# A second out_proj cut in two, with the queries and scores of the gathered block between its halves

## Chip, cores and metric

The kernel runs on one core of one Trainium2 chip. The metric is the device time of one execution in microseconds (us); the lower the better. Three timed runs of the kernel before gave 2075.72, 2077.70 and 2087.32 us, so the median is 2077.7 us. TE below stands for TensorE, the other engines are called as in the profile: PE (TensorE matmul), PEld (its weight loads), DVE (VectorE), ACT (ScalarE), POOL (GpSimd), SP (SyncE, which here only issues DMAs; SPq, ACTq are the queues of those engines).

## What is computed

One layer of a diffusion backbone over 512 latent tokens (four blocks of 128, numbered l = 0 to 3) with a prefix of 256 context tokens. Only its second half matters here. The output of the two token mixers goes through one output projection, then through a layer in which every token fetches 8 x 16 single-neuron experts out of 16384 (PEER):

```python
x = x + gt1 * merge_branches(...)          # the last step in it: y @ w_out, w_out is 1024 x 1024
h2 = rmsnorm(x, norm_ffn) * (1 + sc2) + sh2
# per block of 128 tokens:
q = (hb @ w_q).reshape(128, 8, 2, 64)                       # queries, 8 heads
s = einsum('thpd,hpkd->thpk', q, keys)                      # scores, 2 x 128 keys a head
half_s, half_i = top_k(s, 16)                               # selection, first stage
best_s, best_c = top_k(all 16 x 16 sums, 16)                # selection, second stage
experts = i1 * 128 + i2;  gate = softmax(best_s)
act = gelu(einsum('td,thkd->thk', hb, u_table[experts]))
out = einsum('thk,thkd->td', gate * act, v_table[experts])
```

The result is added to x and normalised. All matmuls of 1024 inputs are done in three products, hi*hi + hi*lo + lo*hi, of a rounded value and its remainder.

## The kernel before, in words

The kernel is written with a tile framework whose scheduler decides the order of the instructions on every engine: it takes what is ready by its own model of time, by priority, else in the order of the program. Each engine then works through its own list strictly in that order. What matters lies between the mixers and the loop over the experts:

- **Order of the program** (before): `out_proj(PAIRS[0])` for blocks 3 and 2, `out_proj(PAIRS[1])` for blocks 0 and 1, `transpose_h2` of the first pair, `queries(PAIRS[0])`, `scores(3)`, `transpose_h2` of the second pair, `run_topk(TK0)`, `queries(PAIRS[1])`, `run_topk(TK1)`, then `scores` of blocks 2, 0 and 1, and after that the loop.
- **out_proj** (L1274): eight steps k of 128 input channels. Each loads 512 KB of w_out into a `w_raw` tile (four buffers), `split` (L164 to L171) rounds it on ACT (L169, `w_hi`) and takes the remainder on POOL (L170, `w_lo`; three buffers each), and PE does 12 matmuls of 512 columns (L174 to L176) into four accumulators `pt`. After the eighth step a chain per block makes h2 of it: DVE L1295 (two products out of PSUM), L1296 (sum with `xr`), ACT L1299 (squares) and L1301 (root), DVE L1300, L1302, L1303 (`junk`) and L1304 (`h2t`).
- **transpose_h2** (L1309): PE L1315 transposes h2t, ACT L1318 rounds the result (`h2T_hi`), DVE L1319 takes the remainder (`h2T_lo`). The matmuls of `queries` read both.
- **queries** (L1322): per head a load of 512 KB of peer_wq in four DMAs, the same split, 24 matmuls of 256 columns, one copy on ACT (L1333).
- **scores** (L1335): per two heads one PSUM tile of scores (L1339), copied by ACT to `sce` (L1341) and stored to `scd` in DRAM (L1342).
- **The selection** `topk` (L1091) reads a block's scores back from `scd` (L1094) into `sc` and works on DVE alone: L1101 to L1105 (first stage), L1108 to L1118 (sums), L1126 to L1130 (second stage), then for each head three instructions of 800 elements (L1137, L1139, L1140) that look up the expert's number. Block LG = 3 is the one whose experts are gathered row by row with indirect DMAs (L1439, L1450); the other three are computed densely. `run_topk(us)` emits as much of the selection as a budget of `us` covers, with high priority: 10 (TK0) and 30 (TK1) before the loop, the rest piece by piece in the loop. These budgets count, they look at no clock: they cover all of block 3's selection but the last seven of its eight look-ups.
- **The loop** over 128 groups of experts begins with L1393 to L1397 (constants into PSUM and a tile), `transpose_u` (L1465 DVE, L1466 ACT, L1470 POOL) and `first_product` (PE, tile `pa`). From L1393 on the order of DVE and POOL is written by hand (`manual_schedule`). L1396 writes into memory that the `sce` tiles held, so it waits until their stores to DRAM have landed.

## Time and profile before

| | us |
|---|---|
| three timed runs | 2075.72, 2077.70, 2087.32 (median 2077.7) |
| the profiled execution, its own time | 2080.87 |
| its span from first to last instruction | 2079.1 |
| PE, DVE, ACT, POOL busy | 1928.9, 1643.1, 951.1, 976.9 |
| mean granted clock of TensorE | 0.969 |
| end of the first half of the second out_proj on PE | 710.1 |
| queries of blocks 3 and 2 on PE | 726.1 to 752 |
| queries of blocks 0 and 1 on PE | 758.4 to 784 |
| selection of block 3 before the loop, on DVE | 766.8 to 797.5 |
| first matmul of the loop | 802.3 |

The busy times are sums over the whole span; the change touches some 110 us of it, from 700 to 802. A row of a timeline reads: start, duration, engine, line, operation, tiles out<-in, shape, count, and in brackets how long the engine had been idle and what ended that wait. The durations of DVE and ACT rows include some 0.06 to 0.1 us in which the next instruction has already begun.

### The profile page before, as it was taken

The numbers are of one execution on the slowest core, as the hardware profiler recorded it, in microseconds if no ns is written. First come the engines' busy times: TensorE is split into PE (matmuls) and PEld (weight loads), VectorE is DVE, ScalarE is ACT, GpSimd is POOL, SyncE is SP. The second block draws the span as 40 slices with busy tenths as digits, with TensorE's granted clock in tenths as the row PEclk, the third lists the DMA queues.
The fourth block names the chain that finished last, engine by engine and source line by source line (L and its number), as shares of the span: only waits on it lengthen the run. The fifth ranks groups of instructions, "written<-read, shape, count | busy, mean of one in ns | idle before, by whom it ended". The sixth has DMA issues, their size and how long they took to land.

```text
span 2079.1 us, 29606 instructions
## 1 busy us (share of the span) xinstructions
PE 1928.9 (93%) x10018; PEld 1627.8 (78%) x10018; DVE 1643.1 (79%) x3304; ACT 951.1 (46%) x1769; POOL 976.9 (47%) x695
## 2 busy tenths in 40 slices
PE   6999999999897897999999999899889999999998
PEld 2766666788786696989999999888778777777786
DVE  4599885378776768799998999666879898989855
ACT  5545544333333443333766666895323333333333
POOL 2655534311212872677565666443445555555200
PEclk9999999999998998999999999999999999999999
DMA  9333322422515685889889878789999999999963
GB/s 308 92 112 116 107 82 81 127 84 63 138 51 182 201 195 158 234 234 252 242 255 266 246 236 256 242 259 309 300 315 376 386 386 393 389 391 397 352 233 107
DMA packets 283477, 475.87 MB, mean 229 GB/s; under 512 B 35224, under 2 KB 197293, under 8 KB 282813
## 3 DMA queue, kind: packets, MB, share of 16 engines
q1 hardware_dynamic: 214251, 277.82, 43.9%
q0 software_dynamic: 36864, 134.23, 18.9%
q10 hardware_dynamic: 32210, 61.93, 8.4%
q8 instruction: 79, 1.29, 0.3%
q14 instruction: 73, 0.60, 0.1%
HBM read 409.71 MB, written 64.18 MB: 228 GB/s over the span
## 4 chain that ended last, share of the span: by engine, by line
PE 36%; DMA 17%; DVE 14%; issue 14%; POOL 12%; ACT 5%; ACTq 1%; SPq 1%; DVEq 0%; POOLq 0%
DMA grow<-in_peer_v_dram,exi 7%; POOL w_lo L1470 7%; POOL grow L1439 3%; PE pg L176 3%; PE pg L175 3%; PE pg L174 3%; PE pacc L175 3%; PE pacc L176 2%; PE pacc L174 2%; PE pa L176 2%; PE pa L174 2%; PE pa L175 2%; DMA rep<-ad 2%; DVE accg L1454 2%; PE pm L1422 2%
## 5 line engine op out<-in xcount | busy, mean ns | idle before, releaser
L1470 POOL TENSOR_TENSOR w_lo<-ut,w_hi 128x512 fp32r<-128x512 f32 x224 | 293.9, 1335 | 231.4 <-ACT w_hi L1466 225.3
L174 PE MATMUL pa<-h2T_hi,w_hi 128*128 128x384 f32 x1024 | 354.6, 346 | 35.2 <-ACT w_hi L1466 32.4
L176 PE MATMUL pa<-h2T_hi,w_lo 128*128 128x384 f32 x1024 | 361.2, 354 | 9.3 <-POOL w_lo L1470 8.4
L175 PE MATMUL pa<-h2T_lo,w_hi 128*128 128x384 f32 x1024 | 349.9, 342 | 0.0
L170 POOL TENSOR_TENSOR w_lo<-w_raw,w_hi 128x1024 fp32r<-128x1024 f32 x78 | 200.1, 2576 | 305.1 <-ACT w_hi L169 229.3
L1450 POOL DMA_INDIRECT grow<-in_peer_v_dram,exi x128 | 200.0, 1563 | 168.0 <-DVE accg L1454 143.4
L1552 ACT CAST w_hi<-w_raw 128x1024 fp32r<-128x1024 f32 x124 | 130.3, 1051 | 226.3 <-DMA w_raw<-in_peer_v_dram 110.8
L175 PE MATMUL pacc<-w_lo,wh 128*128 128x512 f32 x744 | 214.0, 403 | 20.1 <-DVE w_lo L1556 19.5
L174 PEld LDWEIGHTS pa<-h2T_hi,w_hi 128*128 128x128 f32 x1024 | 198.3, 194 | 43.3 <-ACT w_hi L1466 42.8
L176 PEld LDWEIGHTS pa<-h2T_hi,w_lo 128*128 128x128 f32 x1024 | 197.8, 193 | 16.0 <-POOL w_lo L1470 13.1
L176 PE MATMUL pacc<-w_hi,wl 128*128 128x512 f32 x744 | 208.8, 396 | 0.0
L174 PE MATMUL pacc<-w_hi,wh 128*128 128x512 f32 x744 | 208.3, 395 | 0.0
L175 PEld LDWEIGHTS pa<-h2T_lo,w_hi 128*128 128x128 f32 x1024 | 197.5, 193 | 0.3
L1439 POOL DMA_INDIRECT grow<-in_peer_u_dram,exi x128 | 148.3, 1159 | 100.4 <-DVE act L1432 80.4
L175 PEld LDWEIGHTS pacc<-w_lo,wh 128*128 128x128 f32 x744 | 138.6, 190 | 63.0 <-DVE w_lo L1556 31.7
L1466 ACT CAST w_hi<-ut 128x1024 fp32r<-128x1024 f32 x126 | 132.6, 1053 | 114.6 <-DVE ut L1465 80.4
L1454 DVE SCALAR_TENSOR_TENSOR accg<-grow,act,accg 128x1024 f32<-128x1024 f32 x127 | 162.8, 1282 | 25.1 <-DMA grow<-in_peer_v_dram,exi 24.1
L1556 DVE TENSOR_TENSOR w_lo<-w_raw,w_hi 128x1024 fp32r<-128x1024 f32 x124 | 151.3, 1220 | 33.7 <-ACT w_hi L1552 33.7
L176 PEld LDWEIGHTS pacc<-w_hi,wl 128*128 128x128 f32 x744 | 140.6, 189 | 34.3
L174 PEld LDWEIGHTS pacc<-w_hi,wh 128*128 128x128 f32 x744 | 139.4, 188 | 34.7 <-ACT wh L1543 0.5
L1465 DVE STREAM_TRANSPOSE ut<-w_raw 128x1024 f32<-128x1024 f32 x126 | 155.8, 1238 | 10.7 <-DMA w_raw<-in_peer_u_dram 7.9
L174 PE MATMUL pg<-hL_hi,w_hi 128*128 128x512 f32 (+1 forms) x336 | 139.6, 416 | 0.0
(447 smaller groups left out, 4115.9 us busy)
## 6 DMA issues: line engine op xcount, KB each, us to landing
w_raw<-in_peer_u_dram SPq DMA_DIRECT2D x512, 128.0 KB
w_raw<-in_peer_v_dram SPq DMA_DIRECT2D x128, 512.0 KB
Gd<-stg ACTq DMA_DIRECT2D x48, 512.0 KB
gg<-Gd SPq DMA_DIRECT2D x16, 1536.0 KB
Ad<-ga ACTq DMA_DIRECT2D x112, 192.0 KB
aa<-Ad SPq DMA_DIRECT2D x28, 768.0 KB
w_raw<-in_w_ada_dram SPq DMA_DIRECT2D x40, 512.0 KB
w_raw<-in_w_in_dram SPq DMA_DIRECT2D x34, 512.0 KB
```

Of the source, the lines that this page charges most:

```text
L170: (lo_eng or G).tensor_tensor(lo, raw, hi.bitcast(F32), op=ALU.subtract)
L174: PE.matmul(o, lh, rh, start=start, stop=False)
L175: PE.matmul(o, lh, rl, start=False, stop=False)
L176: PE.matmul(o, ll, rh, start=False, stop=stop)
L1439: G.indirect_dma_start(out=u, out_offset=None, in_=UT_, in_offset=bass.IndirectOffsetOnAxis(ap=exi[:, j:j + 1], axis=0))
L1450: G.indirect_dma_start(out=v, out_offset=None, in_=VT_, in_offset=bass.IndirectOffsetOnAxis(ap=exi[:, j:j + 1], axis=0))
L1454: V.scalar_tensor_tensor(accg, v, act[:, j:j + 1], accg, op0=ALU.mult, op1=ALU.add)
L1465: V.transpose(lf.rearrange("p (c f q) -> p c f q", f=4, q=32), u.rearrange("p f (c x) -> p c f x", x=32))
L1466: S.copy(hi, lf)
L1470: eng.tensor_tensor(lo[:, cs], lf[:, cs], hi[:, cs].bitcast(F32), op=ALU.subtract)
L1552: S.copy(vh, v)
L1556: V.tensor_tensor(vl, v, vh.bitcast(F32), op=ALU.subtract)
```

## The change

- `out_proj` takes a range of steps. The second one, for blocks 0 and 1, is done in two calls: steps 0 to 3 before, steps 4 to 7 after `queries(PAIRS[0])` and `scores(3)`. Its four accumulators stay open between the halves; its chain for h2 follows the second half.
- `scores(LG)`: the copies of block 3's scores go from PSUM straight to the tile `sc` of the selection, and the four stores to `scd` and the load from it are gone. The scores of the other blocks still go through `scd`.
- The order of the program becomes: out_proj of 3 and 2, first half of 0 and 1, transposes of 3 and 2, queries of 3 and 2, scores of 3, second half of 0 and 1, transposes of 0 and 1, `run_topk(TK0)`, and on as before.

```diff
--- before.py
+++ after.py
@@ -1064,6 +1064,7 @@
     psa = psa_cm.__enter__()
     psm = [None, None]
     io = [iota]
+    kept = {}
     ready, now, spent, stage = {}, [0], [0.0, 0.0], [0]
     LG = NLB - 1
 
@@ -1090,8 +1091,9 @@
 
     def topk(l):
 
-        sc = tkt([P, HEADS, 2 * KEYS], "sc")
-        SP.dma_start(sc, scd[l])
+        sc = kept[l] if l in kept else tkt([P, HEADS, 2 * KEYS], "sc")
+        if l not in kept:
+            SP.dma_start(sc, scd[l])
         hs = tkt([P, HEADS, 2, TOPK], "hs")
         hi = tkt([P, HEADS, 2, TOPK], "hi", U32)
         yield 0.1
@@ -1271,13 +1273,15 @@
 
         return a.rearrange("p (g c x) -> p c g x", g=4, x=32)
 
-    def out_proj(pair):
-        xs = {}
-        for l in pair:
-            xs[l] = gst([P, D], "xr", bufs=2)
-            SP.dma_start(xs[l], I["x"][0, l * P:(l + 1) * P])
-        acc = {(l, j): psum() for l in pair for j in range(2)}
-        for k in range(KC):
+    def out_proj(pair, ks=(0, KC), state=None):
+
+        xs, acc = state or ({}, {})
+        if not state:
+            for l in pair:
+                xs[l] = gst([P, D], "xr", bufs=2)
+                SP.dma_start(xs[l], I["x"][0, l * P:(l + 1) * P])
+            acc.update({(l, j): psum() for l in pair for j in range(2)})
+        for k in range(*ks):
             raw = raw_tile()
             SP.dma_start(raw, I["w_out"][0, k * P:(k + 1) * P])
             hi, lo = split(raw)
@@ -1286,6 +1290,8 @@
                 for j in range(2):
                     js = slice(j * 512, (j + 1) * 512)
                     mm3(acc[l, j], yT_hi[:, k, ls], yT_lo[:, k, ls], hi[:, js], lo[:, js], k == 0, k == KC - 1)
+        if ks[1] < KC:
+            return xs, acc
         hs = {}
         for l in pair:
             x = xs[l]
@@ -1333,19 +1339,25 @@
             S.copy(qp[:, h, ts], pt[:, :256])
 
     def scores(l):
+        if l == LG:
+            kept[l] = tkt([P, HEADS, 2 * KEYS], "sc")
         for h in range(0, HEADS, 2):
             pt = psum()
             for j in range(2):
                 PE.matmul(pt[:, j * 256:(j + 1) * 256], qp[:, h + j, l * P:(l + 1) * P], keysT[:, h + j], start=True, stop=True)
+            if l == LG:
+                S.copy(kept[l][:, h:h + 2].rearrange("p h f -> p (h f)"), pt)
+                continue
             sce = gst([P, 512], "sce", tag="gA", bufs=3) if h < 4 else gst([P, 512], "sce", tag="yA", bufs=2)
             S.copy(sce, pt)
             S.dma_start(scd[l, :, h:h + 2].rearrange("p h f -> p (h f)"), sce)
 
     hs = out_proj(PAIRS[0])
-    hs1 = out_proj(PAIRS[1])
+    half = out_proj(PAIRS[1], (0, KC // 2))
     transpose_h2(hs)
     queries(PAIRS[0])
     scores(3)
+    hs1 = out_proj(PAIRS[1], (KC // 2, KC), half)
     transpose_h2(hs1)
     run_topk(TK0)
     queries(PAIRS[1])
```

Line numbers move with it: L1101 to L1140 become L1103 to L1142, L1295 to L1333 become L1301 to L1339, the matmul of the scores L1339 becomes L1347, their copy and store L1341 and L1342 become L1352 and L1353 (L1349 is the new copy into `sc`), and the loop's L1393 becomes L1405.

**PE, after the first half of the second out_proj, before.** pt_5919 to pt_5922 are the accumulators of blocks 0 and 1, w_hi_5979 the weights of step 3, w_hi_5997 those of step 4, h2t_5890 the result of block 3.

```order
L176 MATMUL pt_5922<-w_hi_5979,yT_lo_5513 128x512
L174 MATMUL pt_5919<-w_hi_5997,yT_hi_5512 128x512
L174 MATMUL pt_5920<-w_hi_5997,yT_hi_5512 128x512
L174 MATMUL pt_5921<-w_hi_5997,yT_hi_5512 128x512
L174 MATMUL pt_5922<-w_hi_5997,yT_hi_5512 128x512
L1315 MATMUL pt_6091<-cst_91,h2t_5890 128x128 x4
L1315 MATMUL pt_6098<-cst_91,h2t_5890 128x128 x4
L175 MATMUL pt_5919<-w_lo_5998,yT_hi_5512 128x512
```

**The same place after the change**, h2t_5903 being the result of block 2, pt_6032 the queries of the first head:

```order
L176 MATMUL pt_5922<-w_hi_5979,yT_lo_5513 128x512
L1321 MATMUL pt_5995<-cst_91,h2t_5890 128x128 x4
L1321 MATMUL pt_6002<-cst_91,h2t_5890 128x128 x4
L1321 MATMUL pt_6009<-cst_91,h2t_5903 128x128 x4
L1321 MATMUL pt_6016<-cst_91,h2t_5903 128x128 x4
L174 MATMUL pt_6032<-h2T_hi_5735,w_hi_6028 128x256
```

Steps 4 to 7 have moved out from between the transposes of blocks 3 and 2, and PE's list goes straight from step 3 to what needs h2 of these blocks.

**PE, where the second out_proj now ends.** w_hi_6376 are the weights of step 7, pt_6316 the last scores of block 3, h2t_6392 and h2t_6404 the results of blocks 0 and 1, pt_6490 the first head of their queries:

```order
L1347 MATMUL pt_6316<-keysT_5511,qp_5734 128x256 x2
L175 MATMUL pt_5921<-w_lo_6377,yT_hi_5512 128x512
L176 MATMUL pt_5921<-w_hi_6376,yT_lo_5513 128x512
L174 MATMUL pt_5922<-w_hi_6376,yT_hi_5512 128x512
L175 MATMUL pt_5922<-w_lo_6377,yT_hi_5512 128x512
L176 MATMUL pt_5922<-w_hi_6376,yT_lo_5513 128x512
L1321 MATMUL pt_6416<-cst_91,h2t_6392 128x128 x4
L1321 MATMUL pt_6423<-cst_91,h2t_6392 128x128 x4
L1321 MATMUL pt_6430<-cst_91,h2t_6404 128x128 x4
L1321 MATMUL pt_6437<-cst_91,h2t_6404 128x128 x4
L174 MATMUL pt_6490<-h2T_hi_5735,w_hi_6486 128x256
```

Between the last step of the out_proj and the transposes of its own result no other work stands on PE any more.

**DVE, the end of the second pair's chain and the start of the selection, before:**

```order
L1303 SCALAR_TENSOR_TENSOR junk_6084<-xr_5917,r2_5737,a2b_5725 128x1024
L1304 TENSOR_TENSOR h2t_6079<-junk_6084,sh2b_5726 128x1024
L1319 TENSOR_TENSOR h2T_lo_5736<-pt_6423,h2T_hi_5735 128x4x128
L1319 TENSOR_TENSOR h2T_lo_5736<-pt_6430,h2T_hi_5735 128x4x128
L1319 TENSOR_TENSOR h2T_lo_5736<-pt_6437,h2T_hi_5735 128x4x128
L1319 TENSOR_TENSOR h2T_lo_5736<-pt_6444,h2T_hi_5735 128x4x128
L1101 MAX hs_6453<-sc_6451 128x8 x6
```

**The end of the same chain after the change**, for block 1 (h2t_6404), with the selection's tiles bs_6829, bp_6830, cand_6809, sc_6303:

```order
L1131 MAX bs_6829<-cand_6809 128x8 x5
L1308 RECIPROCAL r2_5737<-r2_5737 128x1
L1132 MAX_INDEX bp_6830<-bs_6829,cand_6809 128x8 x8
L1309 SCALAR_TENSOR_TENSOR junk_6409<-xr_5917,r2_5737,a2b_5725 128x1024
L1134 CAST bpf_6831<-bp_6830 128x128
L1310 TENSOR_TENSOR h2t_6404<-junk_6409,sh2b_5726 128x1024
L1139 TENSOR_TENSOR sc_6303<-cst_91,bpf_6831 128x800
L1141 TENSOR_TENSOR sc_6303<-sc_6303,ce_6810 128x800
L1325 TENSOR_TENSOR h2T_lo_5736<-pt_6430,h2T_hi_5735 128x4x128
L1142 TENSOR_REDUCE ef_6832<-sc_6303 128x16
L1325 TENSOR_TENSOR h2T_lo_5736<-pt_6437,h2T_hi_5735 128x4x128
L1405 COPY iop_7002<-cst_91 128x128
```

The chain of blocks 0 and 1 now stands between the pieces of the selection; of the part of the selection that is done before the loop, only L1142 comes after the first L1325 of block 1. From L1405 (before: L1393) on, DVE's list is the same row by row in both kernels; PE's, ACT's and SP's have the same rows in the loop, of which a few have changed places with a neighbour.

## Rows read from the trace of the kernel before

**Rows 1.** The page: its first line, and the chain of work that ended last, as shares of the span.

```profile
span 2079.1 us, 29606 instructions
PE 36%; DMA 17%; DVE 14%; issue 14%; POOL 12%; ACT 5%; ACTq 1%; SPq 1%; DVEq 0%; POOLq 0%
```

**Rows 2.** The chain that ended last, in order of time, from 690 to 870 us (start, us, engine, what).

```profile
751.65 4.20 DMA w_raw<-in_peer_wq_dram
...
758.38 0.70 DVE h2T_lo L1319
...
784.38 9.51 PE pt L1339 x44
794.53 4.27 DMA scd<-sce
802.47 3.03 DMA w_raw<-in_peer_u_dram
```

**Rows 3.** Timeline of PE, 706 to 728 us: steps 3 and 4 of the second out_proj, the transposes of blocks 3 and 2, and the first queries.

```profile
707.28 1.09 PE L174 MATMUL pt<-w_hi,yT_hi 128*128 128x512 f32 x4
...
710.09 1.09 PE L174 MATMUL pt<-w_hi,yT_hi 128*128 128x512 f32 x4
711.87 1.09 PE L1315 MATMUL pt<-cst,h2t 128*128 128x128 f32 x8 [0.70 <-DVE h2t L1304]
...
723.34 1.06 PE L1315 MATMUL pt<-cst,h2t 128*128 128x128 f32 x8 [0.99 <-DVE h2t L1304]
...
726.22 0.28 PE L175 MATMUL pt<-h2T_lo,w_hi 128*128 128x256 f32 x1
726.34 0.28 PE L176 MATMUL pt<-h2T_hi,w_lo 128*128 128x256 f32 x1
```

**Rows 4.** Timeline of DVE, 590 to 860 us: pieces of the two pairs' chains.

```profile
644.59 1.22 DVE L1262 SCALAR_TENSOR_TENSOR a2b<-a2b,nfb 128x1024 f32<-128x1024 f32 x1
...
716.32 0.17 DVE L1302 RECIPROCAL r<-r 128x1 f32<-128x1 f32 x1 [0.89 <-ACT r L1301]
...
719.88 3.31 DVE L1304 TENSOR_TENSOR h2t<-junk,sh2b 128x1024 f32<-128x1024 f32 x1
724.62 0.69 DVE L1319 TENSOR_TENSOR h2T_lo<-pt,h2T_hi 128x512 fp32r<-128x512 f32 x1 [1.43 <-ACT h2T_hi L1318]
...
726.42 1.88 DVE L1295 TENSOR_TENSOR h2t<-pt,gt1b 128x512 f32<-128x512 f32 x3
...
742.85 3.31 DVE L1304 TENSOR_TENSOR h2t<-junk,sh2b 128x1024 f32<-128x1024 f32 x1
...
758.38 1.29 DVE L1319 TENSOR_TENSOR h2T_lo<-pt,h2T_hi 128x512 fp32r<-128x512 f32 x2 [0.18 <-ACT h2T_hi L1318]
```

**Rows 5.** Timeline of POOL: single remainders of weights, in windows of 717 to 720 and of 715 to 745 us.

```profile
718.72 3.39 POOL L170 TENSOR_TENSOR w_lo<-w_raw,w_hi 128x1024 fp32r<-128x1024 f32 x1
...
742.21 2.86 POOL L170 TENSOR_TENSOR w_lo<-w_raw,w_hi 128x1024 fp32r<-128x1024 f32 x1 [0.48 <-ACT w_hi L169]
```

**Rows 6.** The instructions of three lines of DVE, 690 to 800 us (duration in ns: least, median, most; first and last start in us).

```profile
L1296 DVE TENSOR_TENSOR xr<-xr,h2t x4: 1212/2323/3444, 700.5 to 729.4; 128x1024 f32<-128x1024 f32 x4
L1303 DVE SCALAR_TENSOR_TENSOR junk<-xr,r,a2b x4: 1503/2508/3248, 706.0 to 741.3; 128x1024 f32<-128x1024 f32 x4
L1304 DVE TENSOR_TENSOR h2t<-junk,sh2b x4: 3307/3308/3312, 708.5 to 742.8; 128x1024 f32<-128x1024 f32 x4
```

**Rows 7.** DVE, the selection of block 3 and the start of the loop: the busy time of one stretch (us, DVE busy, count, granted clock, DMA share, GB/s), then rows of the timeline.

```profile
766.80:797.50 30.70, 30.50 (x216) 1.00 0.48 153
...
796.62 0.99 DVE L1140 TENSOR_REDUCE ef<-sc 128x16 f32<-128x800 f32 x1
797.52 0.28 DVE L1393 COPY iop<-cst 128x128 f32<-128x128 f32 x1
799.11 0.43 DVE L1396 CAST h<-cst 128x512 bf16<-128x512 f32 x1 [1.30 <-DMA scd<-sce]
```

**Rows 8.** Timeline of PE, 757 to 809 us: queries of blocks 0 and 1, the last scores, the first matmuls of the loop.

```profile
760.19 0.41 PE L174 MATMUL pt<-h2T_hi,w_hi 128*128 128x256 f32 x1
760.40 0.41 PE L175 MATMUL pt<-h2T_lo,w_hi 128*128 128x256 f32 x1
...
784.22 9.66 PE L1339 MATMUL pt<-keysT,qp 128*128 128x256 f32 x44
802.27 0.69 PE L174 MATMUL pa<-h2T_hi,w_hi 128*128 128x384 f32 x1 [8.40 <-ACT w_hi L1466]
```

**Rows 9.** Busy time of each engine in four stretches (us, PE, PEld, DVE, ACT, POOL with counts, granted clock, DMA share, GB/s).

```profile
760.00:770.00 10.00, 10.00 (x73) 10.00 (x73) 3.17 (x19) 3.55 (x5) 3.99 (x2) 0.83 0.49 158
...
800.00:810.00 10.00, 7.39 (x27) 6.88 (x28) 6.58 (x7) 4.70 (x5) 6.92 (x6) 0.60 0.82 173
...
800.00:900.00 100.00, 88.14 (x450) 84.92 (x451) 85.12 (x210) 32.48 (x41) 60.75 (x49) 0.89 0.78 209
...
1600.00:1800.00 200.00, 195.52 (x829) 154.45 (x828) 178.73 (x206) 67.86 (x90) 109.90 (x70) 1.00 1.02 390
```

**Rows 10.** The way of block 3's last scores: the copy of the queries and the copy of the scores on ACT, the store, and the first instruction of the selection on DVE.

```profile
752.71 0.36 ACT L1333 COPY qp<-pt 128x256 f32<-128x256 f32 x1
...
757.25 0.60 ACT L1341 COPY sce<-pt 128x512 f32<-128x512 f32 x1
...
766.83 1.26 DVE L1101 MAX8 hs<-sc 128x8 f32<-128x128 f32 x6 [7.16 <-DMA sc<-scd]
```

## Prediction

> **What bounds the kernel now.** I read the page first: the chain that ended last is spread over PE, DMA, DVE and POOL [rows 1], so there is no single bottleneck, and a change is worth what it does in its own stage. The stage here runs from 700 us to the loop. Next the chain in order of time [rows 2]: before 758.4 it goes through loads of peer_wq, through L1319 of blocks 0 and 1 it enters PE, the last scores on PE follow (to 793.9), then the landing of their stores, then the loop. So in this stage the loop starts when the queries and scores of blocks 0 and 1 are through, and those start when L1319 delivers h2T_lo at 759 us. The selection is not on this chain. DVE works through it without a gap (30.5 busy of 30.7 us) while PE does these queries, and after it still waits 1.30 us for the stores [rows 7]. Ending it earlier buys nothing by itself: L1396 would stand there until 799.1 all the same, and the last product of PE before the loop would be where it is. The question is therefore when, in the changed order, L1325 (L1319 before) delivers blocks 0 and 1.
>
> **1. A hole after the first half.** PE issues step 3 at 707.28 and step 4 at 710.09, one step being 2.81 us [rows 3]. Before, steps 4 to 7 (11.2 us) filled the time in which DVE, ACT and POOL made h2 of blocks 3 and 2; PE's only holes were 0.70 us and 0.99 us ahead of the transposes [rows 3]. Now PE's list has nothing until the transposes, so it idles through that time, and 11.2 us of work wait for later. One gain comes with it. All four L1304 take 3.31 us, while the like L1296 takes 1.21 at best and 3.44 at worst [rows 6]. The reason shows in the times: L1304 at 719.88 ends at 723.19, 1.08 us after the POOL instruction of 718.72 ended (722.11), and the one at 742.85 ends at 746.16, 1.09 us after that of 742.21 (745.07) [rows 4, 5]. DVE stands until POOL's is done. With PE idle, POOL runs out of free w_lo buffers (three) after the third head at about 718.8, so block 2's L1304 should take about 1.2 us, not 3.31. The queries of blocks 3 and 2 need block 2's L1319, whose first half ended at 725.2 (724.62 + 0.6) [rows 4]; minus 2.1 us they start at about 723.1.
>
> The Trainium skill, GPSIMD Engine Reference, "Key points", has GpSimd share its SBUF interfaces with VectorE and names instructions with two SBUF inputs as a case of contention; the rows of L1304 agree where POOL is busy, and none here shows L1304 with POOL idle. Had 3.31 us been L1304's own price, the sum below would be 2.1 us higher for block 2 and 4.2 us higher for blocks 0 and 1.
>
> **2. Queries of blocks 3 and 2.** 8 heads of 24 matmuls at 0.12 us (726.22 to 726.34 [rows 3]) are 23.0 us. Loads and splits have run ahead in the hole and keep up at some 2.4 us a split, so PE is the bound here. After a hole its clock is down: from 760.2 the matmuls came every 0.21 us (1.2 GHz) in place of 0.12 (2.4 GHz), the granted clock of those 10 us being 0.83 [rows 8, 9]. In the first 10 us of the loop, after 8.40 us of idle, it was 0.60; as a mean of 0.5 and 1 that is 8.0 us at the low level, 2.3 of them before the first matmul, so 5.7 us of work. 5.7 us hold 27 matmuls at 0.21, 2.5 us more than at 0.12. So 25.5 us, to 748.6; then a quarter of step 4 that stands ahead of the eighth head (4 x 0.234 = 0.9) and the first pair of score products (44 rows took 9.66 us, four rows a pair: 0.9) [rows 8]. The copies on ACT (0.36, then 0.60 [rows 10]) add 1.0: the selection can begin at **751.5**, 15.3 us earlier than 766.83 [rows 10]. That includes the trip through DRAM, 9.0 us from the end of the copy (757.85) to the first MAX8 [rows 10], which is saved.
>
> **3. The second half, then the exposed chain.** After 750.5, PE has 44 matmuls at 0.234 (10.3) and three pairs of scores (2.6): the out_proj of blocks 0 and 1 ends at 763.4, not 726.1. Its chain on DVE was then hidden by the queries of blocks 3 and 2. Now nothing is left on PE for it to hide behind. And DVE is not free: it is in the selection, whose pieces stand ahead of and between those of the chain, and the list is strictly in order. Ahead of the first L1325 of block 1 stands all of the selection before the loop but L1142, so 30.7 - 1.0 = 29.7 us [rows 7], and of the chain: four L1301 at 0.63 (1.88/3 [rows 4]), two L1302 at 1.21 [rows 6], four small ones at 0.15 [rows 4], two L1309 at 1.22 to 1.50 [rows 4, 6], two L1310 at 1.15, three L1325 at 0.6 [rows 4]: 12.3 us. These are prices with POOL idle, which it should be from about 766 on, with its three buffers full and PE standing. Upper ends: L1302 and L1304 2.2 us more each, L1309 1.8, in all +12.4 for the two blocks [rows 6]. A wait of some 0.6 us is due after the first two heads' 20 instructions (4.8 us), since the second pair of scores stands behind 21 matmuls (750.5 + 4.9 + 0.9 + copy 0.6 = 756.9). Sum: 751.5 + 29.7 + 12.3 + 0.6 = **794.1**, against 759.0 (758.38 + 0.6 [rows 4]): **+35.1 us**. Without the selection the same chain would take from 763.4 its 12.3 us and some 5 us of hops between engines, to 781: 22 us of the loss are the order of the products, 13 the selection.
>
> The Trainium skill, TensorE: Matmul & The Clock Gate, "Architectural detail", says that ScalarE and VectorE work their queues strictly first in, first out; it speaks against an early selection in front of a chain that PE waits for. No row before has such a pile on DVE, so the trace neither shows nor denies it here; if DVE could overtake, the sum would fall by those 13 us.
>
> **4. From there to the end.** Queries and scores of blocks 0 and 1 are the same rows as before; PE has stood 30 us, so I charge 27 matmuls at the slow level where before there were 16 (760.19 to 763.4, rows at 0.21 [rows 8]): 11 x 0.09 = **+1.0 us**. The stores of the last scores, L1393 to L1397, the first transposes: same rows, same distance of 8.4 us on PE [rows 8]. The selection's being done earlier takes 0 off that, because the stores end it [rows 7]. In the loop DVE and POOL have the same lists, and the look-ups left for it are the same seven; nothing is emitted earlier. A few rows of PE and ACT have changed places with neighbours: 0, with ±4 us as my bound, a third of the 11.9 us of PE idle in the loop's first 100 us [rows 9].
>
> **Sum.** 35.1 + 1.0 = +36.1 us on the profiled execution's 2080.87 us: 2117.0. That execution lay 3.2 us above the median of the runs shown, so the median should come to 2113.8, say **2114 us**, 1.7% slower. Its own range: POOL still in the way of the whole chain +12.4, no slow level at either place -3.5 (so 2.5 + 1.0), L1310 at 3.31 +6.3, reordered rows ±4; not all at once: 2106 to 2126.
>
> **The rivals.**
> (a) *The loop gives back part of the delay.* PE idles 11.9 us in the first 100 us of the loop, DVE is 85% busy there [rows 9]; if that idle came from something that does not move with the start, up to 12 us return: about 2102. For it: loads can run ahead in the 30 us hole. Against it: four w_raw buffers bound how far, and DVE's list is the same.
> (b) *The end does not hang on the loop's start.* Between 1600 and 1800 us the DMA share is 1.02 at 390 GB/s [rows 9]. If the transfers there set the end by themselves, the whole delay is absorbed: 2078. Against it: those loads are issued into the same four buffers, one as another is freed, so they move as well; it would need transfers already issued 35 us early.
> (c) *Faster: the selection, not PE, holds the loop.* The mechanism would be DVE's path from L1140 to L1393 (797.52, with no wait [rows 7]) to the loop's first weights; with the selection gone from there PE could go on right after its last scores, saving up to the 8.40 us of idle at 802.27 [rows 8]: 2069. It decides if L1325 of block 1 ends by 759.0 as now; by step 3 the out_proj alone ends at 763.4, and L1396 waits for the stores.
> (d) *The change does less than it says:* if DVE did the chain first, step 3's loss is the 22 us alone: 2101. The list says otherwise; I put it under (a).
>
> **How the numbers follow.** Forecast 0.76; (a) with (d) 0.12; (b) 0.06; (c) 0.06. 0.5% (10.4 us) is about what a measurement of this kernel can tell from no change, so forecast, (a) and (d) are slower (0.88), (b) is the same, (c) faster. The range that should hold 8 in 10 takes the forecast's own, and (a), and a little above: 2098 to 2127.
>
> **What would show it.** In the changed profile: PE idle for some 8 us ahead of block 2's transposes; L1310 of block 2 at 1.2 us; first L1103 near 751.5; the last matmul of the out_proj near 763; PE idle some 30 us until about 794; L1325 between look-ups there; loop start near 838; DVE idle while PE does the queries of blocks 0 and 1. The forecast is wrong if PE's hole before these queries is under 20 us, or if the loop takes less time than the 1276.8 us from 802.3 to the span's end.

## The result, and the profile after

| | us |
|---|---|
| changed kernel, four runs | 2109.49, 2109.84, 2111.34, 2114.04 (median 2110.59) |
| kernel before, four runs | 2075.72, 2077.70, 2083.82, 2087.32 (median 2080.76) |
| ratio of the times | 1.0144, 95% interval 1.011 to 1.0179 |
| predicted for the changed kernel | 2114 (2098 to 2127) |

The change made the kernel 29.8 us slower. The page of the changed kernel, its first line and the chain that ended last by engine [rows 1]:

```profile
span 2107.7 us, 29594 instructions
...
PE 33%; DVE 17%; DMA 15%; issue 14%; POOL 13%; ACT 6%; ACTq 1%; SPq 0%; DVEq 0%; POOLq 0%
```

The span is 28.6 us longer than before. DVE's share of the chain rose from 14 to 17%, PE's fell from 36 to 33%. The chain in order of time (start, us, engine, what) shows where [rows 2]:

```profile
746.08 0.86 DVE hs L1103 x4
...
761.56 1.13 DVE xr L1302
...
778.45 1.15 DVE h2t L1310
779.64 1.97 PE pt L1321 x8
...
808.11 7.78 PE pt L1347 x36
...
817.57 3.92 DMA scd<-sce
```

Before, loads of peer_wq and PE carried this stage. Now, from 746 to 779 us, almost every piece of the chain is DVE, and selection (L1103 to L1132) and chain (L1301 to L1325) alternate in it. Then follow PE's queries and scores and the landing of the stores, as before. (A line L1295 of before is L1301 now, L1303 is L1309, L1304 is L1310, L1319 is L1325, L1396 is L1408.)

PE's timeline, step 3 of the second out_proj, the waits and the loop's first matmul [rows 3, 8]:

```profile
696.32 1.10 PE L174 MATMUL pt<-w_hi,yT_hi 128*128 128x512 f32 x4
...
701.37 1.09 PE L1321 MATMUL pt<-cst,h2t 128*128 128x128 f32 x8 [2.09 <-DVE h2t L1310]
710.35 1.94 PE L1321 MATMUL pt<-cst,h2t 128*128 128x128 f32 x8 [7.88 <-DVE h2t L1310]
712.84 0.58 PE L174 MATMUL pt<-h2T_hi,w_hi 128*128 128x256 f32 x1 [0.55 <-DVE h2T_lo L1325]
...
752.13 0.40 PE L176 MATMUL pt<-w_hi,yT_lo 128*128 128x512 f32 x1
769.58 1.94 PE L1321 MATMUL pt<-cst,h2t 128*128 128x128 f32 x8 [17.05 <-DVE fi L1111]
779.64 1.97 PE L1321 MATMUL pt<-cst,h2t 128*128 128x128 f32 x8 [8.12 <-DVE h2t L1310]
...
824.68 0.69 PE L174 MATMUL pa<-h2T_hi,w_hi 128*128 128x384 f32 x1 [7.93 <-ACT w_hi L1478]
```

PE stood 7.88 us ahead of block 2's transposes, and from the out_proj's last matmul (752.13 + 0.40) to the first query of blocks 0 and 1 at 781.4 it did nothing but two sets of transposes. DVE's timeline beside it [rows 4, 7]:

```profile
705.45 1.47 DVE L1309 SCALAR_TENSOR_TENSOR junk<-xr,r,a2b 128x1024 f32<-128x1024 f32 x1
706.96 3.25 DVE L1310 TENSOR_TENSOR h2t<-junk,sh2b 128x1024 f32<-128x1024 f32 x1
...
740.61 0.87 DVE L1103 MAX8 hs<-sc 128x8 f32<-128x128 f32 x4 [26.97 <-ACT sc L1349]
...
768.23 1.20 DVE L1310 TENSOR_TENSOR h2t<-junk,sh2b 128x1024 f32<-128x1024 f32 x1
...
778.37 1.22 DVE L1310 TENSOR_TENSOR h2t<-junk,sh2b 128x1024 f32<-128x1024 f32 x1
...
781.43 0.68 DVE L1325 TENSOR_TENSOR h2T_lo<-pt,h2T_hi 128x512 fp32r<-128x512 f32 x1
...
817.57 0.29 DVE L1405 COPY iop<-cst 128x128 f32<-128x128 f32 x1 [33.97 <-ACT sce L1352]
821.51 0.43 DVE L1408 CAST h<-cst 128x512 bf16<-128x512 f32 x1 [3.65 <-DMA scd<-sce]
```

POOL [rows 5], block 3's h2g in the timeline, then the two remainders of 703 to 712 us as a group (duration in ns: least, median, most; first and last start in us):

```profile
700.20 3.34 POOL L1312 TENSOR_TENSOR h2g<-junk,sh2b 128x1024 f32<-128x1024 f32 x1
...
L170 POOL TENSOR_TENSOR w_lo<-w_raw,w_hi x2: 2348/2839/3330, 703.5 to 705.8; 128x1024 fp32r<-128x1024 f32 x2
```

The selection starts at 740.61, is cut by the chain and delays it; afterwards DVE stands 33.97 us through all the queries of blocks 0 and 1, and L1408 still waits for the stores (3.65). Busy time in these two stretches (us, PE, PEld, DVE, ACT, POOL with counts, granted clock, DMA share, GB/s) [rows 7, 9]:

```profile
740.61:782.03 41.42, 16.25 (x71) 13.18 (x70) 40.69 (x233) 10.80 (x17) 11.23 (x5) 0.71 0.36 96
784.00:817.00 33.00, 32.74 (x231) 31.15 (x229) 0.00 (x0) 14.22 (x25) 11.90 (x5) 0.98 0.34 106
```

DVE is busy 40.69 of 41.42 us while PE is busy for 16.25; then PE 32.74 of 33 while DVE does nothing. Before, these two ran side by side.

**How to compare two executions.** The stage is counted from the start of step 3 of the second out_proj, since the lists of PE, DVE, ACT and POOL are the same up to there in all kernels of this document (SP's, which issues loads ahead of their use, is not where the out_proj is split); its end is the first matmul of the loop (tile pa). Before it took 802.27 - 707.28 = 95.0 us, now 824.68 - 696.32 = 128.4: **+33.4 us**. The whole span moved by only 28.6, because step 3 began 11.0 us earlier and the rest, from the loop's first matmul to the end, was 6.2 us longer (1283.0, before 1276.8). A second execution of the kernel before (first experiment) shows that neither belongs to the change.

### The profile page after: what moved, and what is told of

Its sections match the earlier page's. It is cut to its first block, busy times and chain, and to the rows that moved or that the text cites. A ratio compares the mean times of both kernels' runs of the same rounds, so it can differ in the third digit from the quotient of the medians.

```text
span 2107.7 us, 29594 instructions
## 1 busy us (share of the span) xinstructions
PE 1927.7 (91%) x10018; PEld 1629.4 (77%) x10018; DVE 1633.6 (78%) x3304; ACT 950.9 (45%) x1769; POOL 974.8 (46%) x695
## 4 chain that ended last, share of the span: by engine, by line
PE 33%; DVE 17%; DMA 15%; issue 14%; POOL 13%; ACT 6%; ACTq 1%; SPq 0%; DVEq 0%; POOLq 0%
POOL w_lo L1482 8%; DMA grow<-in_peer_v_dram,exi 5%; POOL grow L1451 3%; PE pg L176 2%; PE pg L175 2%; PE pg L174 2%; PE pacc L175 2%; PE pacc L176 2%; PE pacc L174 2%; DMA w_raw<-in_peer_v_dram 2%; DVE accg L1466 2%; DMA rep<-ad 2%; PE pa L174 2%; PE pa L176 2%; PE pa L175 2%
## 5 line engine op out<-in xcount | busy, mean ns | idle before, releaser
L1568 DVE TENSOR_TENSOR w_lo<-w_raw,w_hi 128x1024 fp32r<-128x1024 f32 x124 | 151.2, 1219 | 35.1 <-ACT w_hi L1564 35.1
```

The lines of the kernel that those rows point to most:

```text
L1568: V.tensor_tensor(vl, v, vh.bitcast(F32), op=ALU.subtract)
```

## The experiments

Each ratio is against runs of the kernel before on the same chip, whose medians there were 2079.4 to 2080.8 us. Step 3, loop, stage and rest are of one profiled execution each. Times after step 3 are worked out as above from the two rows of PE's timeline.

| run | out_proj of 0, 1 | scores of 3 | selection against the chain | step 3 | loop | stage | rest | median us | ratio (95%) |
|---|---|---|---|---|---|---|---|---|---|
| before | whole | DRAM | behind | 707.28 | 802.27 | 95.0 | 1276.8 | 2080.8 | |
| e0_before_again | whole | DRAM | behind | 697.52 | 792.53 | 95.0 | 1285.0 | 2079.3 (one run) | |
| after | 4 + 4 | copied | mixed | 696.32 | 824.68 | 128.4 | 1283.0 | 2110.6 | 1.0144 (1.011 to 1.0179) |
| e1_chain_first | 4 + 4 | copied | behind | 697.32 | 812.13 | 114.8 | 1283.1 | 2099.0 | 1.0100 (1.0067 to 1.0133) |
| e2_copy_alone | whole | copied | mixed | 702.01 | 799.69 | 97.7 | 1283.2 | 2082.7 | 1.0013 (0.9994 to 1.0032) |
| e3_split_alone | 4 + 4 | DRAM | mixed | 702.89 | 839.55 | 136.7 | 1279.9 | 2121.8 | 1.0215 (1.0179 to 1.025) |
| e4_six_two | 6 + 2 | copied | mixed | 700.78 | 833.95 | 133.2 | 1280.5 | 2115.2 | 1.0176 (1.0137 to 1.0215) |
| e6_copy_chain_first | whole | copied | behind | 704.42 | 794.90 | 90.5 | 1277.6 | 2076.5 | 0.9978 (0.9967 to 0.9989) |
| e9_half_amid_queries | 4 + 4, amid queries | copied | behind | 700.14 | 808.31 | 108.2 | 1279.4 | 2090.9 | 1.0071 (1.0046 to 1.0095) |
| e10_stores_on_pool | whole | DRAM, stores by POOL | behind | 701.88 | 796.83 | 95.0 | 1282.6 | 2080.1 | 1.0006 (0.9985 to 1.0027) |
| e11_copy_chain_first_again | as e6 | | | 703.88 | 794.75 | 90.9 | 1277.4 | 2075.6 | 0.9981 (0.9963 to 0.9999) |
| e5_copy_chain_first_more | as e6, two more look-ups | | | 707.27 | 797.77 | 90.5 | 1293.4 | 2089.6 | 1.0044 (1.0027 to 1.006) |
| e7_more_lookups | as after, all look-ups | | | 703.54 | 837.77 | 134.2 | 1295.3 | 2134.6 | 1.0263 (1.0241 to 1.0286) |

**The kernel before, profiled again.** No edit.

> The kernel before, a second profiled execution. In the first one step 3 of the second out_proj began at 707.3 us, in the changed kernel and four variants of it, whose instructions up to there are the same, at 696.3 to 702.9; from the first matmul of the loop to the end it was 1276.8 us there and 1279.9 to 1283.2 in the others. If both differ from one execution to the next by chance, this one has step 3 at 696 to 703 and a loop of 1278 to 1284 us, with 95 us between the two as before. If the changed loop is longer because of the change, its loop is 1277 us again.

PE's timeline of the second execution, step 3 and the loop's first matmul:

```profile
697.52 1.10 PE L174 MATMUL pt<-w_hi,yT_hi 128*128 128x512 f32 x4
...
792.53 0.69 PE L174 MATMUL pa<-h2T_hi,w_hi 128*128 128x384 f32 x1 [8.05 <-ACT w_hi L1466]
```

The stage is 95.0 us again, while step 3 began at 697.5 and the rest took 1285.0 us (expected 1278 to 1284). So the start of step 3 differs by some 10 us and the rest by some 8 from one execution to the next. Against this execution the changed kernel's span is +30.2: -1.2 before step 3, +33.4 in the stage, -2.0 after it. The loop neither gave anything back nor took more that can be told from chance.

**The selection held behind the chain.** Every L1103 to L1107 uses the tile `hs`, and a copy out of the last block's h2T_lo into it makes them wait:

```diff
         hi = tkt([P, HEADS, 2, TOPK], "hi", U32)
+        if l == LG:
+            V.tensor_copy(hs.rearrange("p h a k -> p (h a k)").rearrange("p (a b) -> p a b", a=2),
+                          h2T_lo[:, 6:8, P:2 * P].bitcast(F32))
```

> The changed kernel, but the selection may begin only after the last L1325 of block 1: one copy (128x256) from h2T_lo into the tile hs stands ahead of it, so all of the selection falls behind the chain on DVE. Everything else is as changed. Theory (22 us of the loss are the order of the products, 13 the selection ahead of the chain on DVE): counted from step 3 of the second out_proj, the last L1325 comes 13 us sooner than in the changed kernel (there 85.7 us after step 3 began, so about 73), the selection then runs beside the queries of blocks 0 and 1 and is through before the loop, and the time is 2110.6 - 13 = 2098 us (2094 to 2102). Rival (the chain's own hops or a busy POOL hold it, the selection only fills its gaps): the last L1325 stays within 3 us of 85.7, and the time is 2110 or a little above, since the selection then ends later. Second rival (the selection is all of the loss): 2080.

DVE's timeline of this kernel (its lines are three higher: L1313 is L1310 of the changed kernel, L1328 is L1325), the end of the chain and the copy:

```profile
769.09 0.69 DVE L1328 TENSOR_TENSOR h2T_lo<-pt,h2T_hi 128x512 fp32r<-128x512 f32 x1 [1.83 <-ACT h2T_hi L1327]
...
770.68 0.29 DVE L1100 COPY hs<-h2T_lo 128x256 f32<-128x256 f32 x1
```

In the expectation "last L1325" stands for its first half in block 1, which ended 85.7 us after step 3 in the changed kernel. Here that is 769.09 + 0.6 - 697.32 = 72.4, and the loop comes 13.6 us sooner (114.8), the time 11.6. The 13 us that the prediction put down to the selection ahead of the chain are shown. The chain's own hops are still there (1.83 for ACT), but they don't hold it.

**The copy alone.** The out_proj in one piece, the rest as changed:

```diff
-    half = out_proj(PAIRS[1], (0, KC // 2))
+    hs1 = out_proj(PAIRS[1])
...
-    hs1 = out_proj(PAIRS[1], (KC // 2, KC), half)
```

> Only the copy of block 3's scores to the selection's tile without DRAM; the second out_proj stands in one piece as before. The order on PE is that of the kernel before; on DVE 31 pieces of the selection now stand ahead of the first L1325 of blocks 0 and 1, and 15 more between the four. Theory (pieces ahead of the chain on an in-order DVE delay it): the scores' first copy ends at about 751 in the times of before, 46 pieces of some 0.24 us and four L1325 of 0.6 end at about 764.5, so the queries of blocks 0 and 1 start some 5 us later than before: 2080.8 + 5 = 2086 us (2082 to 2090). Rival (the copy saves the 9 us by way of DRAM, and this counts): 2072. Rival (the selection is off the path on both sides): 2081, and the queries start as before.

PE's timeline, first queries of blocks 0 and 1:

```profile
752.58 0.38 PE L174 MATMUL pt<-h2T_hi,w_hi 128*128 128x256 f32 x1 [1.22 <-DVE h2T_lo L1325]
756.63 0.58 PE L175 MATMUL pt<-h2T_lo,w_hi 128*128 128x256 f32 x1 [3.67 <-DVE h2T_lo L1325]
```

PE waits 1.22 and 3.67 us for L1325, behind pieces of the selection. The loop starts 2.7 us later than before, not 5, and the time can't be told from before. The direction was right, the price half: the expectation left out that the copy also frees something, which e6 and e10 show below. Against e6, which has the copy too but the selection behind the chain, the pieces ahead of the chain cost 7.2 us (97.7 - 90.5).

**The split alone.** Scores through DRAM as before, out_proj 4 + 4:

```diff
-        if l == LG:
+        if l == LG and False:
             kept[l] = tkt([P, HEADS, 2 * KEYS], "sc")
...
-            if l == LG:
+            if l in kept:
```

> Only the split of the second out_proj; block 3's scores go by way of DRAM as before. Theory: the selection starts some 9 us later than in the changed kernel, block 0's part of the chain is through by then, but 118 rows of the selection still stand ahead of the last L1325 of block 1, so this comes about 9 us later than in the changed kernel (95 us after step 3 began in place of 85.7): 2110.6 + 9 = 2120 us (2114 to 2125). Rival (the order of the products alone sets the loss): 2110, the last L1325 where it was.

PE's timeline, the wait for the last transposes:

```profile
791.31 1.97 PE L1321 MATMUL pt<-cst,h2t 128*128 128x128 f32 x8 [23.08 <-DVE h2t L1310]
```

The stage is 136.7 us, 8.3 longer than changed (forecast 9), the time 11.2. The selection starts later, but its pieces still stand in the list ahead of L1310 of block 1, so PE waits 23.08 us for that one. The copy without DRAM was the better half of the change.

**Six steps ahead and two behind.**

```diff
-    half = out_proj(PAIRS[1], (0, KC // 2))
+    half = out_proj(PAIRS[1], (0, 6))
...
-    hs1 = out_proj(PAIRS[1], (KC // 2, KC), half)
+    hs1 = out_proj(PAIRS[1], (6, KC), half)
```

> The changed kernel with six steps of the second out_proj ahead of the queries of blocks 3 and 2 and two behind, in place of four and four. Theory (behind the scores DVE is the bound, with selection and chain in one list): PE's hole ahead of block 2's transposes is filled by 5.6 us, the second half ends 5.6 us sooner, but the selection starts at the same time and 144 of its rows still stand ahead of the last L1325, so this moves by less than 2 us and the time is 2110 (2107 to 2113). Rival (each step behind the queries costs its own 2.8 us of PE): 2105. Second rival (POOL, with less of a hole to run ahead in, gets in the way of the chain): 2115.

DVE's timeline, the chain of block 2, the first piece of the selection and the second-last L1325:

```profile
710.62 3.21 DVE L1309 SCALAR_TENSOR_TENSOR junk<-xr,r,a2b 128x1024 f32<-128x1024 f32 x1
...
748.04 0.88 DVE L1103 MAX8 hs<-sc 128x8 f32<-128x128 f32 x4 [27.50 <-ACT sc L1349]
...
791.27 0.69 DVE L1325 TENSOR_TENSOR h2T_lo<-pt,h2T_hi 128x512 fp32r<-128x512 f32 x1 [1.83 <-ACT h2T_hi L1324]
```

The rival on PE's time (2105) falls; but so does "no difference": 2115, the stage 4.8 us longer than changed (one execution each; the intervals of the two ratios overlap). Two causes show in the rows, neither tested by a run of its own. L1309 of block 2 takes 3.21 us in place of 1.47, since POOL now works through (four remainders from 708.00 on), and the selection starts 47.3 us after step 3 in place of 44.3. And from its start to the end of block 1's first L1325 it is 43.8 us in place of 41.4, in part because the list has fewer pieces of the selection between the chain's last hops: DVE stands 1.83 us for ACT there. That fewer steps behind the scores don't help is what the theory said; the second rival, POOL in the way, was right about the sign, though for the first pair's chain.

**One piece, copied, selection behind the chain.** The two edits of e1 and e2 together, and once more with more runs.

> The same without the two look-ups: out_proj in one piece, scores copied without DRAM, the selection behind the last L1325 of block 1. Theory (an earlier end of the selection buys nothing by itself, and without pieces of it ahead of the chain the 2.8 us are gone that the copy alone cost): queries and loop start within 1 us of before, 2079.4 us (2077 to 2081). Rival (the trip through DRAM was on the path): 2072.

> The kernel with the out_proj in one piece, the scores copied without DRAM and the selection behind the chain, once more with more rounds, as the fastest version so far. If the gain of 0.22% is real: ratio 0.997 to 0.999 and a loop that starts 90 to 91 us after step 3. If it was chance: a ratio whose interval holds 1.

This is the only version faster than the kernel before, by 4 to 5 us: 0.9978 and 0.9981, both intervals below 1. The loop starts 4.1 to 4.5 us sooner than before, where the theory had "within 1 us". ACT's timeline before, around the copies for the transposes (L1318):

```profile
752.98 1.14 ACT L1341 COPY sce<-pt 128x512 f32<-128x512 f32 x2
755.23 1.02 ACTq L1342 DMA_DIRECT2D scd<-sce  x2
756.29 1.07 ACT L1318 CAST h2T_hi<-pt 128x512 fp32r<-128x512 f32 x2 [2.18 <-PE pt L1315]
```

PE at the same place, the transposes of the first block and the first query of blocks 0 and 1:

```profile
753.76 1.04 PE L1315 MATMUL pt<-cst,h2t 128*128 128x128 f32 x8
...
758.40 0.62 PE L174 MATMUL pt<-h2T_hi,w_hi 128*128 128x256 f32 x3 [2.29 <-ACT h2T_hi L1318]
```

ACT in this kernel (L1352 is the copy of the scores, L1327 is L1318), then PE's first query of blocks 0 and 1:

```profile
749.69 1.17 ACT L1352 COPY sc<-pt 128x512 f32<-128x512 f32 x2
751.14 1.07 ACT L1327 CAST h2T_hi<-pt 128x512 fp32r<-128x512 f32 x2 [0.28 <-PE pt L1324]
```

```profile
753.25 0.62 PE L174 MATMUL pt<-h2T_hi,w_hi 128*128 128x256 f32 x3 [0.40 <-ACT h2T_hi L1327]
```

Before, ACT was through with its copies at 754.1 and the transposes were done at 754.8, but two stores stood ahead of L1318 in ACT's list (L1342, 755.23 to 756.25), so L1318 began at 756.29 and PE waited 2.29 us for it. The issue of a store takes only 0.33 us. What held them is in the chain that ended last of the kernel before, asked for these few us:

```profile
755.87 0.02 ACTq L1342
...
755.92 0.33 ACTq L1342
...
756.29 1.07 ACT h2T_hi L1318 x2
```

What released the piece of 755.87 is the load of peer_wq of 751.65 [rows 2], which landed at 755.85: ACT stood at the second store until a load of weights had landed that neither the store nor L1318 uses. In the trace this store waits for a semaphore on which that load counts its landing, and so does the first store with the load before it. Without stores L1327 follows 0.28 us after the transposes, and PE waits 0.40.

The shorter wait also keeps PE's clock up. After 2.29 us of wait some 16 matmuls came at 0.21 us in place of 0.12, the low level, at a granted clock of 0.83 from 760 to 770 us [rows 8, 9]; that is 16 x 0.09 = 1.5 us. After 0.40 us they come at 0.12 from 754.2 us on. The second execution of before (a wait of 2.64 us, granted clock 0.83 in the 10 us from the first query) and e10 below (0.40 us, 1.00 from 750 to 760 us) show the same. Busy time of this kernel in 10 us from there (columns as above):

```profile
753.00:763.00 10.00, 9.65 (x78) 9.45 (x79) 9.75 (x59) 3.86 (x7) 3.61 (x2) 1.00 0.42 71
```

The 1.9 us of wait and 1.5 us of clock are 3.4 of the 3.8 us by which PE's last scores begin sooner (73.2 us after step 3 in place of 76.9).

**Stores of block 3 issued by POOL**, in the kernel before:

```diff
-            S.dma_start(scd[l, :, h:h + 2]...
+            (G if l == LG else S).dma_start(scd[l, :, h:h + 2]...
```

> The kernel before, with the four stores of block 3's scores issued by POOL in place of ACT. Theory (where the copy without DRAM gains, the selection behind the chain, it gains by ACT's queue: L1342's stores stand ahead of L1318 there, and PE waits 2.3 us for L1318): PE's wait ahead of the queries of blocks 0 and 1 falls from 2.3 to 0.4 us, the loop starts some 3 us sooner after step 3 (92 in place of 95): 2077.5 us (2075 to 2080). Rival (the gain is the trip by way of DRAM, or the selection's earlier end): 95 us, 2080.7. Rival (the stores delay POOL's splits): above 2082.

PE's timeline: the first query of blocks 0 and 1, the last scores, the loop's first matmul:

```profile
751.17 0.62 PE L174 MATMUL pt<-h2T_hi,w_hi 128*128 128x256 f32 x3 [0.40 <-ACT h2T_hi L1318]
...
775.52 9.66 PE L1339 MATMUL pt<-keysT,qp 128*128 128x256 f32 x44
...
796.83 0.69 PE L174 MATMUL pa<-h2T_hi,w_hi 128*128 128x384 f32 x1 [11.64 <-ACT w_hi L1466]
```

DVE's timeline, the start and the end of the selection and L1396:

```profile
762.92 1.26 DVE L1101 MAX8 hs<-sc 128x8 f32<-128x128 f32 x6 [10.48 <-DMA sc<-scd]
...
792.77 0.99 DVE L1140 TENSOR_REDUCE ef<-sc 128x16 f32<-128x800 f32 x1
793.67 0.42 DVE L1396 CAST h<-cst 128x512 bf16<-128x512 f32 x1
```

PE's wait fell to 0.40 as the theory said, and its last scores began 73.6 us after step 3 in place of 76.9 (775.52 - 701.88, 784.22 - 707.28). Yet the loop starts at 95.0 as before: PE now idles 11.64 us ahead of it, and L1396 follows the selection without a wait. So the selection, through DRAM, ends almost together with the scores: with PE 3.3 us sooner it is the bound. The edit has a part in that: with its stores issued by POOL the selection begins 61.0 us after step 3 in place of 59.5 (762.92 - 701.88, 766.83 - 707.28), so up to 1.5 us of the missing gain are its own. Only both together (e6) gave the 4.5 us.

**The second half amid the queries.** As e1, with the second half behind head 3 of the queries of blocks 3 and 2 (`queries` takes a range of heads for it):

```diff
...
-    queries(PAIRS[0])
+    queries(PAIRS[0], range(4))
+    hs1 = out_proj(PAIRS[1], (KC // 2, KC), half)
+    queries(PAIRS[0], range(4, HEADS))
     scores(3)
-    hs1 = out_proj(PAIRS[1], (KC // 2, KC), half)
```

> The split with scores copied without DRAM and the selection held behind the last L1325 of block 1, but the second half of the out_proj stands between heads 3 and 4 of the queries of blocks 3 and 2, so four heads and the scores of block 3 follow it on PE. Theory (the 24 us by which the split alone moves the loop, 114.8 us after step 3 with it and 90.5 without, both with the selection behind the chain, are PE's hole before the queries, some 7 us, its slow clock after that, 2.5, and the chain that nothing on PE covers any more): hole and clock stay, but four heads cover some 13 of the chain's 17 to 20 us, so the loop starts about 106 us after step 3: 2076.5 + 15 = 2091 us (2087 to 2096). Rival (what counts is that four steps come behind the hole, not what stands behind them): 114.8 and 2099 us.

PE's timeline, the last transposes:

```profile
763.29 1.94 PE L1324 MATMUL pt<-cst,h2t 128*128 128x128 f32 x8 [4.19 <-DVE h2t L1313]
```

PE waits 4.19 us for h2t of block 1 and not at all for that of block 0 (in e1 3.67 and 8.16). The loop starts 108.2 us after step 3 (forecast 106), the time is 2090.9 (2091). That the time agrees so closely is luck, since the stage is 2.2 us longer than forecast. Four heads of cover bring back 6.6 us (forecast some 9); the hole ahead of block 2's transposes (7.88) is the same as in the changed kernel.

**More look-ups ahead of the loop.** TK1 36 in the kernel of e6, TK1 60 in the changed kernel.

> The out_proj in one piece as before, block 3's scores copied without DRAM, the selection held behind the last L1325 of block 1 (by the same small copy as above), and two more look-ups of the selection ahead of the loop (TK1 36 in place of 30). Theory (the selection belongs beside the queries of blocks 0 and 1; started 7 us sooner there it has room for two look-ups of 3 us ahead of L1396, which waits for the stores): queries and loop start as before, the loop's DVE has 6 us less to do where it is 85 to 95% busy: 2079.4 - 4 = 2075 us (2072 to 2079). Rival (the loop doesn't hang on DVE's look-ups): 2079.4, no difference. Rival (DVE comes late to L1396): above 2081.

> The changed kernel with all of block 3's look-ups ahead of the loop (TK1 60 in place of 30), in the 34 us in which DVE stands during the queries of blocks 0 and 1. Five more rows of them stand ahead of the last L1325, so the queries start some 4 us later. Theory (the selection's early end pays only if its next work is let in): the loop has 21 us less of DVE's work, of which some 11 come back while it is 85 to 95% busy: 2110.6 + 4 - 11 = 2104 us (2097 to 2110). Rival (the loop doesn't hang on that): 2114. Rival (all 21 come back): 2094.

Both missed, and not by their stages: e5's is that of e6 (90.5; forecast as before, 95), e7's 134.2 is 5.8 us longer than changed, with the pieces ahead of L1325 (forecast some 4). It is the rest that is 1293.4 and 1295.3 us. e5's time fits its last rival (above 2081) by number only, since DVE did not come late: the loop starts as in e6. Sums of busy time over the first 700 us of the loop, e5 and then e6:

```profile
sum 700.00, PE 647.49 PEld 626.24 DVE 588.84 ACT 406.12 POOL 407.08; mean PE 46.25 PEld 44.73 DVE 42.06 ACT 29.01 POOL 29.08
```

```profile
sum 700.00, PE 656.23 PEld 634.02 DVE 600.12 ACT 409.10 POOL 406.15; mean PE 46.87 PEld 45.29 DVE 42.87 ACT 29.22 POOL 29.01
```

PE does 8.7 us less there in e5, and DVE and ACT do less as well (some 6 us of DVE's 11 are the two look-ups that are gone). In both kernels the budgets that run in the loop then take other pieces at other places, so its lists are different ones. Why these lists are worse was not tried further and stays open; that the loop gets faster with each look-up taken out came true in neither kernel.

## Why the prediction came out as it did

The likeliest case came true: the loop's start, not something else, sets the end, and it moved because the chain of blocks 0 and 1 lost its cover on PE and stands in one list with the selection. By its own steps, in us after step 3 began (the forecast's time less 707.28):

| step | forecast | measured |
|---|---|---|
| 1. PE's hole ahead of block 2's transposes | some 8 | 7.88 |
| 1. L1310 of block 2, its duration | 1.2 | 3.25 |
| 1. queries of blocks 3 and 2 start | 15.8 | 16.5 |
| 2. selection starts | 44.2 | 44.3 |
| 3. out_proj of blocks 0 and 1 ends | 56.1 | 56.2 |
| 3. first L1325 of block 1 ends | 86.8 | 85.7 |
| 4. first matmul of the loop | 131.1 | 128.4 |
| the loop's first matmul to the end | 1276.8 | 1283.0 (before: 1276.8 and 1285.0) |

- **Step 1.** The hole was right, L1310 was not: POOL had not run out. It did block 3's h2g first (700.20, 3.34 us) and then two remainders, the second from 705.79 to 709.12, and L1310 ended at 710.21, 1.09 us after it, as in [rows 4, 5]. What made up for most of it is a gain the prediction didn't name: L1309 took 1.47 us in place of 3.25, since it began late in the first remainder (703.5 to 705.8) and ended 1.1 us after that one. So the queries started 0.7 us later than forecast, not 2; that the two errors nearly cancel is luck. In blocks 0 and 1, with POOL idle, L1310 took 1.20 and 1.22. The mechanism was right, POOL's end was put too early: 11.5 us after step 3 (718.8), where it was 12.8. The rule of the Trainium skill that the prediction cited for it (GPSIMD Engine Reference, "Key points") agrees with the rows, POOL busy and idle.
- **Step 3** is the heart of the sum and was mis-sized by 1.1 us of 35.1: 34.0. The parts of the loss are shown: e1 takes the selection from the chain's way and gains 13.6 (forecast 13); what is left against before is 19.8 (forecast 22). That DVE works its list strictly in order, for which the prediction cited the Trainium skill (TensorE: Matmul & The Clock Gate, "Architectural detail"), agrees with e1 and e3.
- **Step 4.** The extra 1.0 us of slow matmuls did not come: about as many query matmuls as before were slow, those up to 785.1 us. The transposes ahead of them ran at the low level as well, 1.97 us for eight in place of 1.06, at a granted clock of 0.50 from 770 to 780 us. From L1325 to the loop it was 42.7 us in place of 43.3. This and step 3 make the 2.7 us by which the stage came out below the sum.
- **The rest.** The forecast stood on one profiled execution. The stage is the same to 0.1 us in two executions of before, but what lies ahead of it and behind it differs by 10 and by 8, in opposite directions in these two. The 6.3 us between the forecast and measured shift of the medians (36.1 and 29.8) are 2.7 of the stage and such spread.
- **Rivals.** (b) is out, the delay came through to the end. (a) is out at its size: with 12 us given back the rest would be 1265 to 1273 us, and it was 1283.0; a few us can't be told from the spread of 8. (d), with the chain first on DVE, is not what the list did, but e1 made it so: 2099 against the 2101 put down for it. (c) is out for this change, where L1408 waits 3.65 us for the stores, but its mechanism is real and near: in e10 PE is 3.3 us sooner and the selection holds the loop at once. "Ending it earlier buys nothing by itself" holds for the kernel before by its rows, and was incomplete.
- **What the prediction missed** is that the copy without DRAM also takes the stores off ACT's queue ahead of L1318. It asked what the DMA costs and not what stands behind its issue. The row was there: the load of peer_wq of 751.65 stands in the chain ahead of L1319 [rows 2], which needs no weights of queries, and the prediction read past it. Without the split, and with the selection behind the chain, that and the earlier selection are worth 4.5 us of the stage (e6). Seen from there the split itself costs 24.3 us (114.8 - 90.5). PE's waits for h2t ahead of its four sets of transposes are 21.8 us in e1 (2.09, 7.87, 8.16, 3.67) and 1.7 in e6 (0.70, 0.99, none, none), so 20.1 of these us are the chains that nothing on PE covers; the other 4 were not taken apart. In the changed kernel the queries wait for DVE, so ACT's freed queue can pay nothing there; what the copy is worth there, 8.3 us (e3), goes with the earlier start of the selection (44.3 us after step 3, 65.8 in e3).

## What to carry to other kernels

A block of matmuls that looks like a delay for what follows it may be the cover for another engine's chain; before moving it, write down what that engine does meanwhile and what PE would have left at that time. On an in-order engine a piece of work that becomes ready earlier goes into the list earlier, ahead of a chain that somebody waits for: start it early only behind that chain (e6), and then the copy without DRAM pays. Where two paths end within a few us of one another, taking one away (e2, e10) shows nothing, and only both together do. A store in the list of a busy engine can stand there until a DMA that has nothing to do with it has landed: ask of each what it waits for, not only how long its issue takes.

## What was not expected of the hardware

- The time up to step 3, with the same lists on PE, DVE, ACT and POOL, ran from 696.3 to 707.3 us over thirteen profiled executions, and from the loop's first matmul to the end, leaving out the two kernels with more look-ups, from 1276.8 to 1285.0; the stage between, twice measured on the kernel before, was 94.99 and 95.01, and on the kernel of e6 and e11 90.5 and 90.9. A change of a few us is read from its stage, not from the span.
- What a busy POOL costs a DVE instruction of 128x1024 with two inputs depends on when it begins: L1309 and L1310 each ended 1.1 us after the POOL instruction beside them (706.9 after 705.8, 710.2 after 709.1), so one took 1.47 us and the next 3.25. POOL's is longer too: the remainder of 705.79 took 3.33 us, the one just before it 2.35. By these ends the two engines took turns: L1309 after the first remainder, the second remainder after L1309, L1310 after that. This is a reading of the rows; no run tests it.
- Two stores in ACT's list cost PE 1.9 us of wait and 1.5 us of low clock though their issue takes 0.33 us each: they stood until loads of peer_wq had landed (755.85).
